# Low halves of every second granule of the up-projections' weights: an adding DMA in place of a subtraction on VectorE

## The chip, the cores and the metric

One core of a Trainium2 chip runs the whole program. The metric is the device time of one execution in microseconds (us), the median of several runs; smaller is better. Times of instructions, waits and transfers come from one profiled execution, whose own time is given beside its span.

## The reference

The program computes a small decoder trunk for 256 tokens of 2048 features in float32: an mLSTM layer, then a layer of differential attention, each followed by a gated feed-forward with a causal convolution over tokens, and a last RMS norm. The change touches the first product of the feed-forward, `xn @ w_up`:

```python
def conv_ffn(xn, w_up, conv_w, conv_b, w_down):
    S = xn.shape[1]
    u = xn @ w_up                       # (256, 2048) @ (2048, 11264)
    up = jnp.pad(u, ((0, 0), (CONV_W - 1, 0), (0, 0)))
    c = conv_b + up[:, 0:S] * conv_w[0]
    for j in range(1, CONV_W):
        c = c + up[:, j:j + S] * conv_w[j]
    gate, val = jnp.split(c, 2, axis=-1)
    return (jax.nn.silu(gate) * val) @ w_down

def reference(x, ...):
    h = x
    for layer in range(DEPTH):          # 2 layers
        ...
        h = h + conv_ffn(rms_norm(h, f_norm[layer]), w_up[layer], conv_w[layer], conv_b[layer], w_down[layer])
    return rms_norm(h, final_norm)
```

## The kernel before

**Products of halves.** A float32 number is split into a high half (rounded to the type `fp32r`, in which TensorE multiplies) and a low half (the number minus its high half). A product is then three: high by high, high by low and low by high. The activations `x` are split once for each layer's norm. The weights are read once and are split as they come.

**Tiles.** `gemm` (from L374) works on 256 columns of a weight matrix at a time, a *pair* of blocks of 128. For each pair it walks over the inner dimension in *granules* of 4 tiles of 128 rows (`HC` = 4). In the up-projection the inner dimension is 2048, so a pair has 4 granules, at `k0` = 0, 4, 8 and 12. A load brings two granules at once: `raw`, 128 partitions by 8 by 256 numbers, 1 MiB (L361). There are five `raw` buffers.

**Splitting a granule** (`granule`, L353 to L372). ScalarE copies the granule's part of `raw` into the high half of a buffer `w2` (L369), which rounds it. VectorE writes the low half as part minus high half (L371). There are five `w2` buffers (`HL` = 5), so the split runs up to four granules ahead of TensorE. In `w2` the high and low half of one tile of rows stand side by side: [128, 4 tiles, 2 halves, 256].

**The matmuls** (L411). For each tile of rows and each block of 128 columns there are two: the high half of the weights against high and low half of `x` side by side (512 wide), and the low half against the high half of `x` (256 wide). A granule of the up-projection has 16 matmuls, a pair 64. When a pair is done, ScalarE and VectorE add up the two halves of each accumulator (L417, L418), and the convolution follows on them (L656 to L673).

**The feed-forward** (`conv_ffn`, from L645). The 5632 hidden features are taken in two halves. For each half there are 22 pairs of the up-projection (11 of the gate, 11 of the value, alternating), then the down-projection. Two layers of two halves make four up-projection stages of 22 pairs: 88 pairs, 352 granules, 176 loads.

**Order and queues.** Every engine works through its own queue in order; the order is set when the program is built. Loads are all issued by SyncE, and wait until the last reader of a `raw` buffer is done. GpSimd issues no transfers. In the profile's names `w` is the tile `w2`, `x_f` the split activations of the feed-forward, `hid` the split hidden features.

Of the kernel before, what the change touches and what calls it, by code (L numbers as in the profile page):

```python
# [45 lines left out]
# 500000 ** (-i / 16) in float32, once for each half of a rotary pair  # L46
# [19 lines left out]
def trunk(  # L66
# [41 lines left out]
    # the tensor engine's clock rises with use: have it up when the first operands come  # L108
# [14 lines left out]
    # mask_a: row q, column k, NEG where k > q; mask_s: row s, column t, NEG where s > t; each twice  # L123
# [10 lines left out]
    def columns(sources, name):  # L134
        """rows of 128 parameters each, transposed: column j has parameters 128 j .. 128 j + 127"""
# [40 lines left out]
    def parameters():  # L176
# [3 lines left out]
        # w_hnorm / 2: the sigmoid of the output gate is (1 + tanh) / 2  # L180
# [7 lines left out]
    class Norm:  # L188
        """Sum of squares over the features, and the operands (h * gain) split in two exact halves."""
# [29 lines left out]
        def first(self, i, ps):  # L219
            """the same from the transposed input"""  # L220
# [11 lines left out]
        def rstd(self):  # L232
            """1 / sqrt(mean square + eps): rt per token on partitions, a column for each half of the tokens; r on every partition"""
# [16 lines left out]
    def sums(a):  # L250
        """the sums of a over the partitions: (P, 2), tokens on partitions, a column for each half of them"""
# [5 lines left out]
    def rsqrt(v, name, eng):  # L257
        """1 / sqrt(v) for (P, 2): a first guess from the exponent, then Newton's steps"""
# [17 lines left out]
    def spread(y):  # L276
        """(P, 2) with tokens on partitions to (P, T) with the same T tokens on every partition"""
# [25 lines left out]
    def split_weights(p, h_at, name):  # L303
        """(128, 384) of weights p[s, t] in two halves: columns 0-255 the first half of s against all t, columns 256-383 the second
        half of s against the second half of t. Three blocks of (h, l), in that order"""
# [11 lines left out]
    def weighted(v, p):  # L317
        """sum over s of p[s, t] v[s, :], a bank with t on partitions for each half of t"""
# [11 lines left out]
    def squares(banks):  # L330
        """the sum of squares of a head's 256 features, (P, 2)"""
# [12 lines left out]
    def turn(rows, name):  # L344
        """two (128 t, 256) to features on partitions, (2, T)"""
# [7 lines left out]
    def granule(w, c0, k0, kn, raws, j, hc=None, first=False, own=True):  # L353
        """the two halves of up to HC k-tiles of 256 columns; a load brings KC of them, at the very beginning HC"""
# [13 lines left out]
        w2 = wpool.tile([P, HC, 2, CW], F32R, tag="w2", name="w2", bufs=HL)  # L368
        splits.append(act.activation(w2[:, :hc, 0], part, AF.Copy))  # L369
        eng = pool if first and k0 // HC % 2 else dve  # L370
        eng.tensor_tensor(w2[:, :hc, 1], part, w2[:, :hc, 0].bitcast(F32), op=ALU.subtract)  # L371
        return [(w2[:, i, 0], w2[:, i, 1]) for i in range(hc)], w2  # L372

    def gemm(xs, w, col0, pairs, evac, tokens_out=False, lead=1, before=None, narrow=()):  # L374
        """256 columns of w at a time. Features out: ps[n] is (128 columns, T). tokens_out: ps[t] is (128 tokens, 256 columns).
        Every product is of two 12-bit halves: wh xh + wh xl + wl xh. wide: the first two are one matmul, of the two halves side by
        side, into the two halves of a bank, which are added up at the end.
        narrow: pairs without that.
        lead: the first so many pairs leave the last operands until all of them have used the others."""
# [7 lines left out]
        for j, k0 in order:  # L387
# [6 lines left out]
            halves, w2 = granule(w, c0, k0, kn, raws, j, ends[k0] - k0, before is not None)  # L394
            wide = j not in narrow
            for i, (wh, wl) in enumerate(halves):
                k = k0 + i
                xh, xl, xhl = xs[k]
                for n in range(2):
                    s = slice(n * P, (n + 1) * P)  # L400
                    one = ps[n][:, :T]
                    if wide and tokens_out:
                        ops = ((xh[:, s], w2[:, i].rearrange("p a n -> p (a n)"), ps[n]), (xl[:, s], wh, one))
# [18 lines left out]
    def gemm_by_tokens(xs, w, col0, evac):  # L422
        """256 columns of w, tokens out, the first half of the tokens ahead of the second"""
        kn, raws, halves = len(xs), {}, []
        ps = [acc_ps.tile([P, 2 * T], F32, tag="acc", name="acc")[:, :T] for _ in range(2)]
        for t in range(2):
            s = slice(t * P, (t + 1) * P)
            for k in range(kn):
                if t == 0 and k % HC == 0:
                    # the first HL granules in the weights' own buffers, the others in blocks that are free by now  # L430
# [36 lines left out]
    def x_squares():  # L467
        """the sum of squares per token"""
# [6 lines left out]
    def mlstm(norm):  # L475
# [5 lines left out]
        def gates():  # L481
            gw = wpool.tile([P, KC * CW], F32, tag="raw", name="gw", bufs=RAW)[:, :KD * 16].rearrange("p (k n) -> p k n", n=16)
            # the columns' first halves and, 64 columns on, their second halves
# [450 lines left out]
```

## Time and profile before

| | us |
|---|---|
| median of 3 runs | 2281.04 (2280.92 to 2281.47) |
| span of the profiled execution | 2280.0 |
| TensorE busy | 2267.8 |
| VectorE busy | 1588.7 |
| ScalarE busy | 1258.4 |
| GpSimd busy | 175.7 |
| DMA engines, mean rate | 183 GB/s |

The span is the time from the first to the last instruction of one profiled execution. PE is TensorE's matmuls, PEld its weight loads, DVE VectorE, ACT ScalarE, POOL GpSimd, SP SyncE; a "q" behind a name is the engine's sequencer. A row of the groups shows line, engine, operation, what is written from what, the shape and the count, then the busy time in all, the mean time of one in ns, and the engine's idle time just before with what ended it. A row of the busy times by stage shows the stretch, then the busy time and the count for each engine, then TensorE's granted clock, the busy share of the 16 DMA engines and their rate in GB/s. A row of the timeline shows start, duration and instruction, with the idle time before it in brackets.

### The profile page before, as it was taken

The page shows a single profiled execution, that of the slowest core. Times are in us where ns is not written, and L with a number is a line of the kernel's source. Part 1 is how long each engine was busy: PE and PEld are TensorE (multiplying, and loading weights), DVE is VectorE, ACT ScalarE, POOL GpSimd, SP SyncE. Part 2 cuts the span into 40 slices and gives each one's busy share as a digit, 9 for nine tenths or more (in the row PEclk, how much of TensorE's full clock was granted, in tenths as well). Part 3 has the DMA queues.
Part 4 walks back from the last instruction along what each step waited for, and adds up shares of the span by engine and source line. Part 5 has one row for each costly group of instructions (what it writes and reads, how often), then busy time and mean ns, then how long its engine had stood idle before and what let it go on. Part 6 is the DMA issues. An engine that isn't in the chain of part 4 may idle for free.

```text
span 2280.0 us, 34236 instructions
## 1 busy us (share of the span) xinstructions
PE 2267.8 (99%) x13318; PEld 1995.3 (88%) x13318; DVE 1588.7 (70%) x2667; ACT 1258.4 (55%) x2019; POOL 175.7 (8%) x379
## 2 busy tenths in 40 slices
PE   9999999999999999999999999999999999999998
PEld 8888888888888888888988888988888888888887
DVE  7756667777764677775588875677777556777755
ACT  6466555655554455655554556556555445555544
POOL 2023001000000000000122213210000000000000
PEclk9999999999999999999999999999999999999999
DMA  9654566555556655565656555555555565555552
GB/s 281 186 151 150 181 187 193 185 194 188 185 178 192 202 187 185 188 190 175 200 184 191 167 159 162 179 185 185 188 192 185 171 198 192 189 191 192 174 184 89
DMA packets 415783, 418.18 MB, mean 183 GB/s; under 512 B 9134, under 2 KB 415620, under 8 KB 415620
## 3 DMA queue, kind: packets, MB, share of 16 engines
q1 hardware_dynamic: 415620, 415.98, 57.6%
q8 instruction: 105, 1.72, 0.3%
q14 instruction: 58, 0.48, 0.1%
HBM read 413.86 MB, written 2.10 MB: 182 GB/s over the span
## 4 chain that ended last, share of the span: by engine, by line
PE 99%; DMA 1%; SPq 0%; DVE 0%; ACT 0%; issue 0%; DVEq 0%; ACTq 0%
PE acc L411 95%; PE val_ps L326 1%; PE acc L435 1%; DMA raw<-in_m_w_in_dram 0%; PE as_ps L759 0%; DMA x_raw<-in_x_dram 0%; PE w_ps L572 0%; PE gps L492 0%; PE as_ps L760 0%; PE hn_ps L350 0%; PE an_ps L350 0%; PE s_ps L579 0%; PE out_ps L863 0%; PE t_ps L781 0%; SPq L361 0%; SPq L460 0%
## 5 line engine op out<-in xcount | busy, mean ns | idle before, releaser
L371 DVE TENSOR_TENSOR w<-raw,w 128x1024 fp32r<-128x1024 f32 (+1 forms) x799 | 957.9, 1199 | 563.4 <-ACT w L369 560.5
L369 ACT ACTIVATE w<-raw 128x1024 fp32r<-128x1024 f32 (+1 forms) x803 | 833.1, 1038 | 759.8 <-PE acc L411 717.2
L411 PE MATMUL acc<-x_f,w 128*128 128x512 f32 (+1 forms) x5632 | 985.1, 337 | 0.0
L411 PEld LDWEIGHTS acc<-x_f,w 128*128 128x128 f32 x5632 | 861.0, 188 | 122.0
L411 PE MATMUL acc<-hid,w 128*128 128x512 f32 (+1 forms) x2772 | 481.5, 335 | 0.0
L411 PEld LDWEIGHTS acc<-hid,w 128*128 128x128 f32 x2772 | 420.4, 188 | 57.8
L417 ACT ACTIVATE low<-acc 128x256 f32<-128x256 f32 x354 | 129.6, 384 | 188.6 <-PE acc L411 188.3
L418 DVE TENSOR_TENSOR acc<-acc,low 128x256 f32<-128x256 f32 x354 | 138.4, 430 | 71.1 <-ACT low L417 71.1
L411 PE MATMUL acc<-x_a,w 128*128 128x256 f32 (+1 forms) x1056 | 186.0, 335 | 1.3 <-ACT w L369 0.7
L411 PE MATMUL acc<-x_at,w 128*128 128x512 f32 (+1 forms) x1024 | 181.5, 338 | 0.0
L411 PEld LDWEIGHTS acc<-x_a,w 128*128 128x128 f32 x1056 | 160.2, 190 | 22.9 <-DVE w L371 1.0
L411 PEld LDWEIGHTS acc<-x_at,w 128*128 128x128 f32 x1024 | 156.7, 188 | 21.9
L658 ACT ACTIVATE c<-u,conv 128x256 f32<-128x256 f32 x176 | 95.7, 592 | 0.0
L411 PE MATMUL acc<-w,x_a 128*128 128x512 f32 (+1 forms) x512 | 93.4, 340 | 0.0
L411 PE MATMUL acc<-w,x_at 128*128 128x256 f32 (+1 forms) x544 | 93.1, 329 | 0.0
L411 PE MATMUL acc<-ao,w 128*128 128x512 f32 (+1 forms) x576 | 91.0, 319 | 0.0
L411 PE MATMUL acc<-mo,w 128*128 128x256 f32 (+1 forms) x544 | 90.3, 327 | 0.0
L411 PEld LDWEIGHTS acc<-ao,w 128*128 128x128 f32 x576 | 81.7, 188 | 8.6
L411 PEld LDWEIGHTS acc<-mo,w 128*128 128x128 f32 x544 | 80.0, 188 | 9.8
L411 PEld LDWEIGHTS acc<-w,x_at 128*128 128x128 f32 x544 | 80.3, 188 | 9.2
L411 PEld LDWEIGHTS acc<-w,x_a 128*128 128x128 f32 x512 | 78.4, 188 | 10.7
L659 DVE SCALAR_TENSOR_TENSOR c<-u,conv,c 128x255 f32<-128x255 f32 x176 | 76.9, 478 | 0.0
(255 smaller groups left out, 1159.4 us busy)
## 6 DMA issues: line engine op xcount, KB each, us to landing
raw<-in_w_up_dram SPq DMA_DIRECT2D x176, 1024.0 KB
raw<-in_w_down_dram SPq DMA_DIRECT2D x64, 1024.0 KB
raw<-in_m_w_in_dram SPq DMA_DIRECT2D x46, 1024.0 KB
raw<-in_w_kv_dram SPq DMA_DIRECT2D x32, 1024.0 KB
raw<-in_w_down_dram SPq DMA_DIRECT2D x32, 768.0 KB
raw<-in_m_w_out_dram SPq DMA_DIRECT2D x16, 1024.0 KB
raw<-in_w_q_dram SPq DMA_DIRECT2D x16, 1024.0 KB
raw<-in_w_o_dram SPq DMA_DIRECT2D x16, 1024.0 KB
```

The source lines that it names most:

```text
L326: pe.matmul(ps[:, :vh.shape[1]], a, b, start=(s == 0 and o == 0), stop=(s == t and o == 2))
L369: splits.append(act.activation(w2[:, :hc, 0], part, AF.Copy))
L371: eng.tensor_tensor(w2[:, :hc, 1], part, w2[:, :hc, 0].bitcast(F32), op=ALU.subtract)
L411: pe.matmul(to, a, b, start=(k == 0 and o == 0), stop=(k == kn - 1 and o == len(ops) - 1))
L417: act.activation(low, p[:, T:], AF.Copy)
L418: dve.tensor_tensor(p[:, :T], p[:, :T], low, op=ALU.add)
L435: pe.matmul(ps[t], a[:, s], b, start=(k == 0 and o == 0), stop=(k == kn - 1 and o == 2))
L658: act.activation(c, u, AF.Identity, bias=cw[:, 3, f:f + 1], scale=cw[:, 2, f:f + 1])
L659: dve.scalar_tensor_tensor(c[:, 1:], u[:, :T - 1], cw[:, 1, f:f + 1], c[:, 1:], op0=ALU.mult, op1=ALU.add)
```

## The change

Three edits go together.

1. The buffer `w2` is laid out by half first: [128, 2 halves, 4 tiles, 256]. All stages use it. Where the tokens are the output's rows, the 512-wide operand is now two runs of 256 numbers that lie 4 KB apart.
2. In the four up-projection stages, every second granule (`k0` = 4 and 12, the second granule of each `raw`) gets its low half in another way: ScalarE writes the negated rounded part into the low half, and GpSimd issues a transfer that adds the part from `raw` to it.
3. The other granules of these stages, and all granules of the other stages, are split as before.

```diff
-        w2 = wpool.tile([P, HC, 2, CW], F32R, tag="w2", name="w2", bufs=HL)
-        splits.append(act.activation(w2[:, :hc, 0], part, AF.Copy))
-        eng = pool if first and k0 // HC % 2 else dve
-        eng.tensor_tensor(w2[:, :hc, 1], part, w2[:, :hc, 0].bitcast(F32), op=ALU.subtract)
-        return [(w2[:, i, 0], w2[:, i, 1]) for i in range(hc)], w2
+        w2 = wpool.tile([P, 2, HC, CW], F32R, tag="w2", name="w2", bufs=HL)
+        high, low = w2[:, 0, :hc], w2[:, 1, :hc]
+        splits.append(act.activation(high, part, AF.Copy))
+        if by_dma and k0 // HC % 2:
+
+            act.activation(low, part, AF.Copy, scale=-1.0)
+            pool.dma_start(low, part, accum_op=ALU.add)
+        else:
+            eng = pool if first and k0 // HC % 2 else dve
+            eng.tensor_tensor(low, part, high.bitcast(F32), op=ALU.subtract)
+        return [(w2[:, 0, i], w2[:, 1, i]) for i in range(hc)], w2
...
-                        ops = ((xh[:, s], w2[:, i].rearrange("p a n -> p (a n)"), ps[n]), (xl[:, s], wh, one))
+                        ops = ((xh[:, s], w2[:, :, i], ps[n]), (xl[:, s], wh, one))
...
-                gemm(norm.sets[0], w_up[layer], part * half * P, [j], evac_gate)
-                gemm(norm.sets[0], w_up[layer], D_FF + part * half * P, [j], evac_val)
+                gemm(norm.sets[0], w_up[layer], part * half * P, [j], evac_gate, by_dma=True)
+                gemm(norm.sets[0], w_up[layer], D_FF + part * half * P, [j], evac_val, by_dma=True)
```

ScalarE's queue in the first up-projection stage, one pair and the start of the next. L369 copies the high halves, L417 takes the upper half of an accumulator, L658 is the convolution, L291 splits the hidden features. Before:

```order
L417 ACTIVATE low<-acc 128x256 x2
L369 ACTIVATE w_4805<-raw 128x4x256
L658 ACTIVATE c<-u,conv_4043 128x256 x2
L369 ACTIVATE w_4824<-raw 128x4x256
L369 ACTIVATE w_4845<-raw 128x4x256
L291 ACTIVATE hid_4686<-c 128x256
L291 ACTIVATE hid_4696<-c 128x256
L369 ACTIVATE w_4864<-raw 128x4x256
L417 ACTIVATE low<-acc 128x256 x2
```

The same place with the change, where L370 is the high-half copy, L373 the negated one, L423 and L664 what L417 and L658 were:

```order
L423 ACTIVATE low<-acc 128x256 x2
L370 ACTIVATE w_4815<-raw 128x1024
L664 ACTIVATE c<-u,conv_4043 128x256 x2
L370 ACTIVATE w_4834<-raw 128x1024
L373 ACTIVATE w_4834<-raw 128x1024
L291 ACTIVATE hid_4694<-c 128x256
L291 ACTIVATE hid_4704<-c 128x256
L370 ACTIVATE w_4856<-raw 128x1024
L370 ACTIVATE w_4875<-raw 128x1024
L373 ACTIVATE w_4875<-raw 128x1024
L423 ACTIVATE low<-acc 128x256 x2
```

Each second granule's copy is followed at once by its negation; the evacuations and the split of the hidden features keep about their places around the copies.

SyncE's queue in the same stage, with what each load waits for. DVE and Activation stand for instructions of VectorE and ScalarE, DMAHW for an earlier transfer of SyncE's own, DMASW for one that GpSimd issued. Before:

```order
L361 DMA raw<-in_w_up_dram 128x8x256 [waits DMAHW5_49,DVE_49]
L361 DMA raw<-in_w_up_dram 128x8x256 [waits DMAHW6_49,DVE_49]
L361 DMA raw<-in_w_up_dram 128x8x256 [waits DMAHW7_49,DVE_49]
L361 DMA raw<-in_w_up_dram 128x8x256 [waits DMAHW0_49,DVE_49]
L361 DMA raw<-in_w_up_dram 128x8x256 [waits DMAHW1_49,DVE_49]
```

The same loads with the change:

```order
L361 DMA raw<-in_w_up_dram 128x8x256 [waits DMASW6_49,DMAHW5_49,DVE_49,Activation_49]
L361 DMA raw<-in_w_up_dram 128x8x256 [waits DMASW7_49,DMAHW6_49,DVE_49,Activation_49]
L361 DMA raw<-in_w_up_dram 128x8x256 [waits DMASW0_49,DMAHW7_49,DVE_49,Activation_49]
L361 DMA raw<-in_w_up_dram 128x8x256 [waits DMASW1_49,DMAHW0_49,DVE_49,Activation_49]
L361 DMA raw<-in_w_up_dram 128x8x256 [waits DMASW2_49,DMAHW1_49,DVE_49,Activation_49]
```

A load into a `raw` buffer now also waits for the adding transfer that reads this buffer. GpSimd's queue gets the 176 transfers themselves (L374), each behind the negated copy of its granule.

More of the change, by code (lines that the diff above doesn't have):

```diff
@@ L351, in turn, with granule @@
         return ps
-    def granule(w, c0, k0, kn, raws, j, hc=None, first=False, own=True):
+    def granule(w, c0, k0, kn, raws, j, hc=None, first=False, own=True, by_dma=False):
         at, hc = k0 % KC, hc or min(HC, kn - k0)
@@ L367, in granule, with gemm @@
             return pairs, None
-        w2 = wpool.tile([P, HC, 2, CW], F32R, tag="w2", name="w2", bufs=HL)
-        splits.append(act.activation(w2[:, :hc, 0], part, AF.Copy))
-        eng = pool if first and k0 // HC % 2 else dve
-        eng.tensor_tensor(w2[:, :hc, 1], part, w2[:, :hc, 0].bitcast(F32), op=ALU.subtract)
-        return [(w2[:, i, 0], w2[:, i, 1]) for i in range(hc)], w2
-    def gemm(xs, w, col0, pairs, evac, tokens_out=False, lead=1, before=None, narrow=()):
+        w2 = wpool.tile([P, 2, HC, CW], F32R, tag="w2", name="w2", bufs=HL)
[8 more added lines that the diff above has]
+        return [(w2[:, 0, i], w2[:, 1, i]) for i in range(hc)], w2
+    def gemm(xs, w, col0, pairs, evac, tokens_out=False, lead=1, before=None, narrow=(), by_dma=False):
         kn = len(xs)
@@ L393, in gemm @@
                 before(k0, ends[k0])
-            halves, w2 = granule(w, c0, k0, kn, raws, j, ends[k0] - k0, before is not None)
+            halves, w2 = granule(w, c0, k0, kn, raws, j, ends[k0] - k0, before is not None, by_dma=by_dma)
             wide = j not in narrow
```

## The prediction

> **What bounds the kernel now.** I read the page first, then the busy time by stage, then the timeline of one pair of column blocks, then SyncE's own waits.
>
> ```profile
> span 2280.0 us, 34236 instructions
> PE 2267.8 (99%) x13318; PEld 1995.3 (88%) x13318; DVE 1588.7 (70%) x2667; ACT 1258.4 (55%) x2019; POOL 175.7 (8%) x379
> ...
> PE 99%; DMA 1%; SPq 0%; DVE 0%; ACT 0%; issue 0%; DVEq 0%; ACTq 0%
> ```
>
> TensorE is busy for 2267.8 of 2280.0 us, and the chain that ended last is 99% matmuls. VectorE, whose work the change takes away, does not appear in that chain at all. The change acts in the four up-projection stages (two layers, two halves of the hidden features each); their busy times, one row for each stage and the sum:
>
> ```profile
> core 0: us, PE busy (x) PEld busy (x) DVE busy (x) ACT busy (x) POOL busy (x), PEclk, DMA share, GB/s
> 401.60:648.50 246.90, 246.90 (x1424) 216.59 (x1424) 187.36 (x327) 148.84 (x226) 1.80 (x2) 1.00 0.57 186
> 771.90:1017.20 245.30, 245.30 (x1411) 215.15 (x1410) 183.02 (x301) 143.13 (x217) 0.00 (x0) 1.00 0.57 187
> 1527.10:1774.30 247.20, 247.20 (x1419) 216.28 (x1418) 185.74 (x315) 145.25 (x220) 1.81 (x2) 1.00 0.57 185
> 1897.80:2144.10 246.30, 246.30 (x1411) 215.38 (x1410) 183.33 (x301) 143.45 (x217) 0.00 (x0) 1.00 0.58 186
> sum 985.70, PE 985.70 PEld 863.40 DVE 739.45 ACT 580.67 POOL 3.61; mean PE 246.43 PEld 215.85 DVE 184.86 ACT 145.17 POOL 0.90
> ```
>
> In these stages TensorE is never idle (985.70 of 985.70 us) and runs at the full granted clock (1.00). No faster other engine can shorten them. What can happen is that something else becomes slower than TensorE. Work is paced per load of 1 MiB (two granules); the page counts them:
>
> ```profile
> raw<-in_w_up_dram SPq DMA_DIRECT2D x176, 1024.0 KB
> ```
>
> 985.7 / 176 = **5.60 us of TensorE for each load**, 2.80 us for each granule. The DMA engines are at a share of 0.57: 0.57 x 5.60 = 3.19 us of each 5.60 are taken. The change adds to these engines and to ScalarE.
>
> **The change part by part.** Prices of the compute instructions:
>
> ```profile
> L371 DVE TENSOR_TENSOR w<-raw,w 128x1024 fp32r<-128x1024 f32 x764 | 933.3, 1222 | 559.3 <-ACT w L369 558.3
> L369 ACT ACTIVATE w<-raw 128x1024 fp32r<-128x1024 f32 x764 | 808.4, 1059 | 716.9 <-PE acc L411 678.4 <-issue 19.0 <-DMA raw<-in_m_w_in_dram 5.7
> ```
>
> *Removed:* 176 subtractions of 1.222 us, 215 us of VectorE. It was waiting for ScalarE between them (558.3 us in the row) and nobody on the path waited for it: gain 0.
>
> *Added on ScalarE:* 176 negated copies of the same shape, 176 x 1.06 = 187 us. In the stages ScalarE goes from 580.67 to 767 of 985.70 us, 78%. It keeps up; queued behind a negation are the next high-half copy and the evacuations of the accumulators, each up to 1.06 us later, and both have slack: the high-half copies start when TensorE frees a buffer, four granules before they are read. Cost 0 by itself; if that lead were gone it would be up to the whole 187 us.
>
> *Added on the DMA engines:* 176 accumulating transfers of 512 KiB (one granule, 4 KB in each partition), issued by GpSimd, which does next to nothing there (3.61 us), so nothing is queued behind it. The trace of before has neither an adding transfer nor one from GpSimd. That it uses the same engines is likely, since the page gives every queue as a share of the same 16:
>
> ```profile
> q1 hardware_dynamic: 415620, 415.98, 57.6%
> q8 instruction: 105, 1.72, 0.3%
> q14 instruction: 58, 0.48, 0.1%
> ```
>
> For the price of moving bytes I take the stretch in the middle of one load, where the engines are saturated:
>
> ```profile
> 901.60:904.20 2.60, 2.60 (x16) 2.27 (x16) 1.05 (x1) 1.06 (x1) 0.00 (x0) 1.00 1.03 357
> ```
>
> At 357 GB/s a load of 1.049 MB takes **2.94 us**. An adding transfer has three streams: the source is read, the old destination is read, the sum is written. For a load one read and one write run together as one pass, so bounds for the added transfer are: one pass of 512 KiB, 1.47 us, if the extra read costs nothing; two passes, 2.94 us, if the two reads follow one another; three passes, 4.41 us, if the write does not overlap either. I take **two passes, 2.94 us**: a load is read through one stream that is full at 357 GB/s, and there are twice as many bytes to read here. Then the engines need 2.94 + 2.94 = 5.88 us for each 5.60 us of TensorE. The excess is 0.28 us, 176 x 0.28 = **49 us**. The store of five raw and five split buffers covers only the first loads of a stage.
>
> *The wait that moves.* SyncE's loads are released by the last reader of a raw buffer:
>
> ```profile
> SPq L361 <- DVE w L371: 1372.6, 269, 10.8
> ```
>
> Now every second reader is the adding transfer, so in these stages a load leaves some microseconds later, once the transfer has landed. Behind it on SyncE's queue stand only the next loads. Five raw buffers hold 5 x 5.60 = 28 us of work, so this delay alone is hidden; when the engines are too slow it is the place where it shows.
>
> *The new latency.* One granule's split before:
>
> ```profile
> 903.13 1.06 ACT L369 ACTIVATE w<-raw 128x1024 fp32r<-128x1024 f32 x1 [1.73 <-PE acc L411]
> 904.22 1.23 DVE L371 TENSOR_TENSOR w<-raw,w 128x1024 fp32r<-128x1024 f32 x1 [1.56 <-ACT w L369]
> 905.47 6.18 SPq L361 DMA_DIRECT2D raw<-in_w_up_dram  x2
> ```
>
> ScalarE starts at 903.13, released by TensorE, the low half is there at 905.45, 2.3 us later, and SyncE's next load leaves at 905.47. TensorE reads it four granules, 11.2 us, after the release. Now two copies (2.12 us) and the transfer stand there. The nearest row for a transfer's whole latency is the last store, 256 KB, which follows this last row of the chain:
>
> ```profile
> 2275.07 0.39 DVE stream L893
> ```
>
> From its end, 2275.46, to the end of the span are 4.5 us, issue and landing included. The adding transfer has up to 1 MiB to read instead: 0.79 MB more at 357 GB/s, 2.2 us. In all 2.1 + 4.5 + 2.2 = 8.8 us, under 11.2: hidden on engines that are free, by 2.4 us; with a load in between (2.94 us) 11.8, which is not. That is the third rival below.
>
> *The buffers' layout* (all high halves, then all low halves) changes the addresses that every stage's matmuls read, not their number or shapes. Four stages of the same code take 245.3 to 247.2 us, 1.1 us or less from their mean; I take 0, with 4 x 1.1 = 4.5 us to either side.
>
> Sum: 2280.0 + 49 = 2329.0 us for a profiled execution; the median of the runs before is 1.0 us above its profile (2281.04), so **2330 us**.
>
> **The rivals.** *All hidden, not slower (2281 us).* It needs under 5.60 - 2.94 = 2.66 us of the engines for each adding transfer. For it: the one-pass bound gives 4.41 us a load, 79% of TensorE's time, and a packet here can be a partition's 4 KB, where the loads' are of 1 KB (415.98 MB in 415620 packets). Against it: the second read has to cost less than 81% of a pass.
>
> The Trainium skill, Collectives: The Full Stack, section The bandwidth ceiling: the fold count and why AG ≠ RS ≠ AR, states that the DMA engine's add itself is free and that a reduction runs at half a copy's rate because of its two source reads, about 31 GB/s for each engine and source. By that figure the 32 KiB of an engine would be an estimated 2.1 us, and 2.94 + 2.1 = 5.0 us would be hidden: 2281 us. No run here shows it yet.
>
> *The adding is slower than its reads (2589 us).* With three passes a load needs 7.35 us, 1.75 too many, 176 x 1.75 = 308 us. For it: a read-modify-write that cannot overlap. Against it: loads overlap read and write now.
>
> *Latency, not throughput (2323 us).* The engines have room, but the chain of 11.8 us is longer than the lead. A split buffer's cycle is then 2.8 us of reading plus 11.8, 14.6 instead of 5 x 2.8 = 14.0 us; 0.6 us for every five granules, 352 / 5 x 0.6 = 42 us. It decides only where the engines are not full; ScalarE's evacuations ahead of a copy make it worse.
>
> The Trainium skill, SBUF — State Buffer, section SBUF: two separate sides, adds that GpSimd cannot write a transfer's descriptors while VectorE runs in a mode that takes both ports. By it each transfer could start up to one VectorE instruction later, an estimated 1.2 us more of latency. VectorE's row above (1222 ns for 1024 elements, 1.2 ns each) does not suggest such a mode.
>
> *Faster (2271 us).* The layout suits TensorE's reads, and all its 2267.8 us shrink by what separates the fastest of the four stages from their mean (245.30 and 246.43, 0.46%): 10 us. Nothing in the rows speaks for it, and there is nothing else to win.
>
> **How the numbers follow.** Forecast (two passes) 0.40, all hidden 0.28, slow adding 0.17, latency 0.10, faster 0.05. Changes of 0.2% (4.6 us) count as a difference here. Slower by more: 0.40 + 0.17 + 0.10 = 0.67; within: 0.28; faster: 0.05. The forecast's own range is 2290 to 2418 us: its upper end prices both passes by the stage's mean share instead, 3.19 us a load, so 6.38 us, 0.78 too many, 137 us. The range of all cases, 2278 to 2540 us, holds the forecast, the hidden case and the latency; it leaves out most of the slow adding and the faster case, under 0.2.
>
> **What would show it.** If the forecast holds, the DMA share in the four windows rises from 0.57 to 0.95 or more, TensorE has idle time there that ends on the adding transfers, each stage takes 256 to 261 us instead of 246, and all other stages keep their times. A share of 0.85 with unbroken TensorE time means the second read was cheap. Idle TensorE with a share under 0.9 means latency. It is wrong if the transfers from GpSimd use something other than these 16 engines, or if one takes under 2.66 us of them.

## The result and the profile after

| | before | changed |
|---|---|---|
| median, us (five runs of each) | 2281.04 (2280.92 to 2281.47) | 2289.31 (2288.75 to 2292.71) |
| ratio, 95% interval | | 1.0038 [1.0025, 1.0052] |
| span of the profiled execution, us | 2280.0 | 2287.6 |

The change makes the kernel slower by 8.3 us, more than the 0.2% that can be told apart. The direction was forecast, the size was not: 8 us where 49 were worked out. (The table ahead of the prediction speaks of three runs of the kernel before; with the two taken beside the changed kernel there are five, with the same median.)

The page of the changed kernel, in the lines shown before:

```profile
span 2287.6 us, 35028 instructions
PE 2272.4 (99%) x13318; PEld 1996.0 (87%) x13318; DVE 1385.4 (61%) x2491; ACT 1419.7 (62%) x2195; POOL 330.1 (14%) x555
...
q1 hardware_dynamic: 415620, 415.98, 56.5%
q0 software_dynamic: 25344, 92.29, 21.6%
...
PE 95%; DMA 3%; issue 1%; SPq 0%; DVE 0%; ACT 0%; DVEq 0%; POOLq 0%; ACTq 0%
```

VectorE lost 203 us of work and ScalarE gained 161, and neither shows in the time. A new queue, `q0`, holds the adding transfers: 25344 packets, 144 for each of the 176 (128 of 4 KB and 16 of 4 bytes), and 21.6% of the engines' span. The chain of waits, 99% TensorE before, is now 95% TensorE and 3% DMA.

The busy times by stage, each from just before its first matmul to just behind its last:

```profile
400.20:649.20 249.00, 248.35 (x1424) 216.88 (x1423) 137.61 (x281) 186.20 (x268) 38.38 (x45) 1.00 1.04 276
772.40:1020.90 248.50, 247.27 (x1411) 215.56 (x1410) 133.26 (x258) 183.04 (x260) 37.02 (x43) 1.00 1.04 275
1530.70:1780.80 250.10, 248.30 (x1422) 216.64 (x1421) 137.65 (x273) 183.54 (x262) 38.65 (x45) 1.00 1.04 275
1903.80:2151.80 248.00, 247.09 (x1411) 215.61 (x1410) 133.57 (x258) 183.43 (x260) 37.00 (x43) 1.00 1.04 276
```

The engines' share went from 0.57 to 1.04, and the clock stayed at 1.00. That looks like full engines, and yet a stage takes some 2 us more, not 10 to 15. The groups of the up-projections' matmuls say how much of that is waiting. Before:

```profile
L411 PE MATMUL acc<-x_f,w 128*128 128x512 f32 (+1 forms) x5632 | 985.1, 337 | 0.0
```

and changed, with the adding transfers' own row:

```profile
L417 PE MATMUL acc<-x_f,w 128*128 128x256 f32 (+1 forms) x5632 | 989.5, 337 | 4.3 <-DMA w<-raw 4.1
L417 PEld LDWEIGHTS acc<-x_f,w 128*128 128x128 f32 x5632 | 861.6, 188 | 129.9 <-DMA w<-raw 6.9
...
L374 POOL DMA_DIRECT2D w<-raw x176 | 151.7, 862 | 1073.6 <-ACT w L373 592.2
```

The matmuls hold 4.4 us more busy time and 4.3 us of idle time, nearly all of the idle time ended by an adding transfer. The modelled end of a matmul hides part of a gap in "busy", so I count by the matmuls' starts, here and in the table of the experiments. A matmul of 512 columns is followed by the next start after some 232 ns, one of 256 after some 118 ns. What goes over that by more than 60 ns is called a gap; the rest I call the ordinary distances. The four stages have 7.0 us of gaps (0.3 before), and their ordinary distances are 2.3 us longer. Together the stages grow by 9.1 us. The first of them starts 1.25 us earlier (400.31, was 401.56), and the work between the third and the fourth is 0.3 us shorter. The difference is the span's 7.6 us. The early start is not the transfers' doing: with the layout alone (run 1 below) the first stage starts at 400.57.

Where two of the gaps come from, in the chain of waits of the changed kernel (start, duration, what):

```profile
789.78 2.46 PE acc L417 x14
792.24 0.03 POOLq L374
792.27 2.29 issue
794.55 0.01 POOLq L374
794.57 9.81 DMA w<-raw
804.37 0.04 issue
804.42 1.67 PE acc L417 x8
...
1668.13 9.22 DMA w<-raw
1677.35 0.04 issue
1677.39 2.73 PE acc L417 x15
```

The transfer that leaves at 794.57 lands 9.81 us later. TensorE freed its buffer at about 792.24, so the whole split took 12.1 us, against a lead of 11.2. All 176 together:

```profile
DMA to landing us min/median/max: 4.5/7.8/10.4
```

With the 2.4 us from the release to the issue (two copies and 0.3 us to GpSimd) the split takes 6.9, 10.2 and 12.8 us: most fit into the lead of 11.2, a few don't. SyncE's loads now wait for the adding transfers, as the prediction said, and no gap in these stages ends on a load of weights:

```profile
SPq L361 <- DMA w<-raw: 917.9, 175, 11.4
```

### The profile page after: what moved, and what is told of

The parts are those of the page before. It is cut to its first block, busy times and chain, and to the rows that moved or that the text cites. A ratio compares the mean times of both kernels' runs of the same rounds, so it can differ in the third digit from the quotient of the medians.

```text
span 2287.6 us, 35028 instructions
## 1 busy us (share of the span) xinstructions
PE 2272.4 (99%) x13318; PEld 1996.0 (87%) x13318; DVE 1385.4 (61%) x2491; ACT 1419.7 (62%) x2195; POOL 330.1 (14%) x555
## 3 DMA queue, kind: packets, MB, share of 16 engines
q0 software_dynamic: 25344, 92.29, 21.6%
## 4 chain that ended last, share of the span: by engine, by line
PE 95%; DMA 3%; issue 1%; SPq 0%; DVE 0%; ACT 0%; DVEq 0%; POOLq 0%; ACTq 0%
PE acc L417 92%; DMA w<-raw 2%; PE val_ps L326 1%; PE acc L441 1%; DMA raw<-in_m_w_in_dram 0%; PE as_ps L765 0%; DMA x_raw<-in_x_dram 0%; DMA rows<-in_conv_w_dram 0%; PE w_ps L578 0%; PE gps L498 0%; PE as_ps L766 0%; PE an_ps L350 0%; PE hn_ps L350 0%; PE s_ps L585 0%; PE out_ps L869 0%
## 5 line engine op out<-in xcount | busy, mean ns | idle before, releaser
L370 ACT ACTIVATE w<-raw 128x1024 fp32r<-128x1024 f32 (+1 forms) x803 | 832.9, 1038 | 666.4 <-PE acc L417 609.9
L377 DVE TENSOR_TENSOR w<-raw,w 128x1024 fp32r<-128x1024 f32 (+1 forms) x623 | 742.3, 1192 | 518.8 <-ACT w L370 516.2
L417 PE MATMUL acc<-x_f,w 128*128 128x256 f32 (+1 forms) x5632 | 989.5, 337 | 4.3 <-DMA w<-raw 4.1
L417 PEld LDWEIGHTS acc<-x_f,w 128*128 128x128 f32 x5632 | 861.6, 188 | 129.9 <-DMA w<-raw 6.9
L417 PE MATMUL acc<-hid,w 128*128 128x512 f32 (+1 forms) x2772 | 481.6, 335 | 0.0
L417 PEld LDWEIGHTS acc<-hid,w 128*128 128x128 f32 x2772 | 420.3, 188 | 57.9
L374 POOL DMA_DIRECT2D w<-raw x176 | 151.7, 862 | 1073.6 <-ACT w L373 592.2
L423 ACT ACTIVATE low<-acc 128x256 f32<-128x256 f32 x354 | 130.1, 385 | 130.7 <-PE acc L417 130.4
L417 PE MATMUL acc<-x_a,w 128*128 128x256 f32 (+1 forms) x1056 | 185.2, 335 | 0.2 <-DVE w L377 0.2
L373 ACT ACTIVATE w<-raw 128x1024 fp32r<-128x1024 f32 x176 | 183.5, 1042 | 0.0
L417 PE MATMUL acc<-x_at,w 128*128 128x512 f32 (+1 forms) x1024 | 181.5, 338 | 0.0
L417 PEld LDWEIGHTS acc<-x_a,w 128*128 128x128 f32 x1056 | 159.9, 190 | 21.4 <-DVE w L377 0.6
L417 PEld LDWEIGHTS acc<-x_at,w 128*128 128x128 f32 x1024 | 156.6, 188 | 21.9
L664 ACT ACTIVATE c<-u,conv 128x256 f32<-128x256 f32 x176 | 95.8, 592 | 0.2 <-DVE u L662 0.2
L417 PE MATMUL acc<-w,x_a 128*128 128x512 f32 (+1 forms) x512 | 93.4, 340 | 0.0
L417 PE MATMUL acc<-w,x_at 128*128 128x256 f32 (+1 forms) x544 | 93.1, 329 | 0.0
L417 PE MATMUL acc<-ao,w 128*128 128x512 f32 (+1 forms) x576 | 91.0, 319 | 0.0
L417 PE MATMUL acc<-mo,w 128*128 128x256 f32 (+1 forms) x544 | 90.5, 328 | 0.0
L417 PEld LDWEIGHTS acc<-ao,w 128*128 128x128 f32 x576 | 81.7, 188 | 8.6
L417 PEld LDWEIGHTS acc<-mo,w 128*128 128x128 f32 x544 | 80.1, 188 | 9.8
L417 PEld LDWEIGHTS acc<-w,x_at 128*128 128x128 f32 x544 | 80.3, 188 | 9.2
```

The source lines that it names most:

```text
L370: splits.append(act.activation(high, part, AF.Copy))
L373: act.activation(low, part, AF.Copy, scale=-1.0)
L374: pool.dma_start(low, part, accum_op=ALU.add)
L377: eng.tensor_tensor(low, part, high.bitcast(F32), op=ALU.subtract)
L417: pe.matmul(to, a, b, start=(k == 0 and o == 0), stop=(k == kn - 1 and o == len(ops) - 1))
L423: act.activation(low, p[:, T:], AF.Copy)
```

## The experiments

Eleven kernels, each compared with the kernel before on the same chip (2280.7 to 2281.0 us there). Lengths of the four stages in us, from the starts of their matmuls in the traces, against before:

| kernel | median | ratio | stages, us more than before | gaps over 60 ns |
|---|---|---|---|---|
| changed | 2289.31 | 1.0038 | +1.8 +3.1 +2.7 +1.5 | 7.0 |
| 1 layout alone | 2280.79 | 1.0001 | 0 0 0 0 | 0.3 |
| 2 plain copy | 2284.26 | 1.0015 | +0.4 +1.4 +0.4 +0.2 | 0.5 |
| 3 pieces of 1 KB | 2321.08 | 1.0175 | +10.8 +13.7 +13.1 +7.7 | 42.8 |
| 4 all granules | 2678.94 | 1.1754 | | 401 |
| 5 negations, no transfer | 2281.16 | 1.0001 | -0.3 0 0 0 | 0.3 |
| 6 every fourth granule | 2281.41 | 1.0003 | 0 0 0 0 | 0.4 |
| 7 six split, four raw buffers | 2287.53 | 1.0027 | +0.7 0 +3.8 0 | 4.9 |
| 8 five split, four raw buffers | 2300.05 | 1.0084 | +4.4 +7.0 +2.6 +2.9 | 14.8 |
| 9 late pairs alone | 2284.85 | 1.0019 | +1.6 +0.7 +1.7 +2.6 | 5.1 |
| 10 early pairs alone | 2285.61 | 1.0021 | +2.1 +1.1 +0.4 +1.1 | 4.6 |
| 11 order alone | 2285.79 | 1.0022 | +2.2 +2.5 +0.2 +0.2 | 0.3 |

The last two columns come from one profiled execution of each kernel. It need not be a typical one: run 9's is the slowest of its eleven (2287.49 us), and the executions of runs 7 and 8 spread over 7 and 12 us.

### 1. The layout alone

```diff
-                gemm(norm.sets[0], w_up[layer], part * half * P, [j], evac_gate, by_dma=True)
+                gemm(norm.sets[0], w_up[layer], part * half * P, [j], evac_gate, by_dma=False)
```

(and the same for the value pairs)

> The change without its transfers: new layout of the split buffers, all low halves subtracted by VectorE. Theory 'late transfers' (the changed kernel loses its 8 us where TensorE waits for adding transfers, 7.0 us in 21 gaps of the trace, and the layout costs nothing): 2279 to 2282 us. Rival 'layout' (the new addresses slow the matmuls; they pace 0.7 ns slower in the changed kernel, 983 to 985 us over the stages): 2283 to 2289 us.

2280.79 us, ratio 1.0001 [0.9992, 1.001]. All four stages have their old length to 0.01 us. The layout costs and brings nothing, so the loss belongs to the transfers and what comes with them.

### 2. A plain copy in place of the adding one

```diff
-            pool.dma_start(low, part, accum_op=ALU.add)
+            pool.dma_start(low.bitcast(F32), part)
```

> The 176 transfers copy the raw granule over the negated half instead of adding it, so the low halves are wrong (they hold the whole weight); instructions and their order are those of the changed kernel. Theory 'two reads' (an adding packet of 4 KB takes 328 ns of an engine because both operands are read): a packet takes 150 to 190 ns, the DMA share in the stages falls from 1.04 to about 0.8, the gaps go, 2279 to 2283 us. Rival 'one transfer from GpSimd costs the same whatever it does': packets of about 328 ns, 2289 us.

2284.26 us, ratio 1.0015 [1.0007, 1.0024], 1.3 us above the range of 'two reads'. The queue and one stretch in the first stage:

```profile
q0 software_dynamic: 25344, 92.29, 10.4%
```

```profile
460.00:640.00 180.00, 180.00 (x1031) 157.54 (x1030) 97.61 (x194) 133.85 (x194) 16.94 (x32) 1.00 0.85 281
```

Same packets, same bytes, same 281 GB/s, and half the time: 10.4% of 2281.6 us over 176 transfers is 1.35 us of every engine for each, where the adding one takes 21.6% of 2287.6 over 176, 2.81 us. A single 4 KB packet takes 159 ns plain and 328 ns adding (medians; eight of them on each engine). So adding costs a second pass. That it is the second read which takes it would fit the ratio; no run separates the read from the adding itself. With the short transfer the gaps are gone (0.5 us). About 2 us are left in the distances between matmuls; run 11 is about those. The profiled execution, the fastest of its eleven, has a span of 2281.6 us, 2.6 us more than run 1's on the same chip (2279.0), and 2.3 of them lie in the four stages. The 0.6 us from there to the median are not placed.

### 3. Pieces of 1 KB

```diff
-            pool.dma_start(low, part, accum_op=ALU.add)
+            pool.dma_start(low, part, accum_op=ALU.add, max_dma_last_dim=1024)
```

> The same adding transfers cut into packets of 1 KB instead of 4 KB, same order of instructions. Theory 'at the edge' (8 packets x 328 ns = 2.63 us of each engine for an add, and 2.94 us for a load, 5.57 us in all against 5.60 us of TensorE): any more engine time now shows in full. If an adding packet of 1 KB takes twice a load's 46 ns, 92 ns, an add takes 32 x 92 ns = 2.94 us, the sum is 5.88 us, and the kernel loses 176 x 0.28 = 49 us more or less: 2320 to 2340 us. Rival 'latency alone' (the engines have room, only the wait of single transfers hurts): under 2300 us.

2321.08 us, ratio 1.0175 [1.0159, 1.0191]. That is inside the range of 'at the edge', but by luck, as the page and the waits show:

```profile
span 2324.4 us, 35028 instructions
...
q0 software_dynamic: 92928, 92.29, 25.7%
```

```profile
PEld acc L417 <- DMA w<-raw: 44.0, 63, 2.5
PE acc L417 <- DMA w<-raw: 22.8, 33, 2.1
```

The same bytes in packets of 1 KB, 102 ns each, take 25.7% of 2324.4 us over 176, 3.39 us of an engine, 0.6 us more. The 0.6 us cost 0.23 us for each load (40.3 / 176): the rest still fitted. So the changed kernel has spare time on the engines, though little of it. By the expectation's own sum, with the 102 ns that were measured, an add would take 3.26 us and the kernel would lose 0.60 us for each load, 106 us; it lost 40.

### 4. Every granule by an adding transfer

```diff
-        if by_dma and k0 // HC % 2:
+        if by_dma:
```

> All 352 granules of the four stages get their low half by an adding transfer. Theory 'at the edge': a load and two adds need 2.94 + 2 x 2.63 = 8.20 us against 5.60, so 176 x 2.60 = 458 us more, about 2740 us. Rival 'latency alone': with twice the transfers, each issued earlier or later as before, not over 2350 us. ScalarE is at 93% then and stays below TensorE's time.

2678.94 us, ratio 1.1754 [1.1738, 1.177]. The queue, and the chain of waits by line (cut off by the view at its end):

```profile
q0 software_dynamic: 50688, 184.57, 34.6%
```

```profile
by line: PE acc L417 46.8%; DMA raw<-in_w_up_dram 42.1%; DMA raw<-in_w_down_dram 2.2%; DMA w<-raw 1.8%; issue 1.4%; PE val_ps L326 0.6%; ACT w L370 0.6%; PE acc L441 0.6%; DMA rows<-in_conv_w_dram 0.5%; PE as_ps L765 0.3%; DMA rows<-in_kv_n
```

Now the loads themselves are late: 42% of the chain. 398 us over 176 loads are 2.26 us, where 2.60 were expected. A load and two adding transfers need 5.60 + 2.26 = 7.86 us; an adding one here is 34.6% of 2685.7 us over 352, 2.64, and so 2.58 us are left for the load, or less if waits other than the engines have a part. (The granted clock fell to 0.943 in this run; the adding packets kept their 327 ns.) Run 3 gives 5.83 - 3.39 = 2.44 in the same way. Both are estimates, for packets of the two queues can run side by side on one engine, and the subtraction takes them one after the other. A load with the engines to itself is hardly faster than the prediction had it: in run 4 the loads move at most some 360 GB/s over 6 us, with next to nothing else on the engines, and that is 2.9 us for each.

### 5. The negation without the transfer

```diff
-            pool.dma_start(low, part, accum_op=ALU.add)
+            dve.tensor_tensor(low, part, high.bitcast(F32), op=ALU.subtract)
```

> ScalarE still writes the negated half in every second granule, but VectorE then makes the low half by subtraction and no transfer is issued. It asks what slows the matmuls by 2 us over the four stages (983.2 to 985.1 us by their pitch) in the changed kernel and in the one with plain transfers. Theory 'transfers' (the pitch falls when the DMA engines move more in SBUF): 983 us of pitch, 2280 to 2281.5 us. Rival 'ScalarE' (its extra writes do it): 985 us of pitch, 2282 to 2284 us.

2281.16 us, ratio 1.0001 [0.9992, 1.0009]. ScalarE's 176 negations cost nothing, in the matmuls' distances neither. That leaves the transfers, or what comes with them; runs 7 and 11 tell these apart.

### 6. Half as many adding transfers

```diff
-        if by_dma and k0 // HC % 2:
+        if by_dma and k0 // HC == 3:
```

> Only the last granule of each pair is made by an adding transfer: 88 instead of 176. Theory 'nearly full engines' (the gaps come because loads and adds together leave the engines a few per cent of room, so an add that is issued into a load queues for microseconds): the engines have 1.3 us more room for each load, the gaps nearly go, half of the pitch loss stays, 2281 to 2283 us. Rival 'every add is late when it meets a load' (the gaps scale with the number of transfers): half of the loss stays, 2284 to 2286 us.

2281.41 us, ratio 1.0003 [0.9995, 1.0012], and the transfers land sooner:

```profile
DMA to landing us min/median/max: 4.5/5.8/8.3
```

The longest split is then 2.4 + 8.3 = 10.7 us, inside the lead of 11.2, and TensorE waits nowhere. The ordinary distances, of whose growth half was expected to stay, are as before (984.7 us, 984.9 before). 88 adding transfers are free (ten of the eleven executions lie between 2280.8 and 2281.9 us, one at 2287.61); the loss isn't a price for each transfer.

### 7 and 8. One more split buffer

Run 7 has six split buffers and four raw ones (each of them holds 1 MiB). Run 8 is its control, with four raw buffers and the usual five.

```diff
-RAW = 5
+RAW = 4
-HL = 5
+HL = 6
```

> Six split buffers and four raw buffers instead of five and five: the split runs one granule further ahead, 2.8 us more time for each add. Theory 'latency at the start of the stages' (the longest adds land 10.4 us after their issue, the lead less the two copies is about 9 us): the gaps of 7 us go, 2281 to 2284 us. Rival 'throughput' (the engines are too slow on average): the gaps only come later, 2287 to 2292 us.

> Control for the run before: four raw buffers, the split buffers stay at five. Theory 'latency': as the changed kernel or a little worse, 2287 to 2294 us, since the lead of the split is the same. If this alone is at 2284 us or under, the raw buffers and not the lead made the difference: fewer loads are then in the queues ahead of an add.

Run 7: 2287.53 us, ratio 1.0027 [1.0018, 1.0036]. Run 8: 2300.05 us, 1.0084 [1.0072, 1.0097]. Run 7 missed the range of 'latency' (2281 to 2284 us) and lies in that of 'throughput'. Its trace speaks for latency all the same. Of its 4.9 us of gaps 1.0 lie at the very start of the first stage, where TensorE waits for the convolution's parameters and for no adding transfer, and 3.6 at one place in the third stage:

```profile
1666.00:1672.00 6.00, 4.17 (x15) 3.44 (x15) 5.62 (x11) 4.31 (x7) 1.72 (x2) 0.72 0.62 93
```

There TensorE waits 2.1 us for the 114th adding transfer, which leaves late for a reason of its own (see runs 9 and 10), and then the granted clock falls for 3.4 us, 0.72 in the mean of this stretch, which stretches the distances by another 1.5 us. The changed kernel pauses as long at its 114th transfer and keeps its clock at 1.00; what makes the difference is not shown. All other gaps of run 7 together are 0.3 us: with one granule more of lead no other adding transfer is late.

Against the control, with equal raw buffers, the sixth split buffer, 2.8 us of lead, takes back 12.5 us of the median. In the traces these are 9.9 us of gaps (14.8 to 4.9) and 2.5 us of ordinary distances, since the order on TensorE differs too (run 11). So the transfers' latency against the lead makes the gaps. The control was expected near the changed kernel's own time, at 2294 us at most, and missed that by 6 us, so the fifth raw buffer carries some of the load too. Six split and five raw buffers were not tried.

### 9 and 10. Only the late pairs, only the early pairs

In the changed kernel most gaps lie in the first 50 us behind a stage's first adding transfer. Is it the start of the stage, or the start of the transfers? So the adding transfers were kept out of the first six of a stage's 22 pairs (run 9), or allowed there alone (run 10):

```diff
-                gemm(norm.sets[0], w_up[layer], part * half * P, [j], evac_gate, by_dma=True)
+                gemm(norm.sets[0], w_up[layer], part * half * P, [j], evac_gate, by_dma=j >= 3)
```

(and the same for the value pairs; `j < 3` in run 10)

> The changed kernel with adding transfers only from the seventh of a stage's 22 pairs on (128 transfers instead of 176); the first 6 pairs, 34 us, are split by VectorE as before. Theory A (the gaps belong to the start of a stage, where the loads come in bursts and an adding transfer queues behind them): at most half of the changed kernel's 7.0 us of gaps is left, 3 us or less, and with the other order on TensorE (up to 2 us) the time is 2281 to 2285 us. Theory B (a start of its own: the adding transfers need some loads until they fall into step, wherever they begin): the gaps only move behind the first transfers, 5 to 8 us in all, and the time stays at 2286 to 2290 us.

> The other part alone: adding transfers only in the first 6 of a stage's 22 pairs (48 transfers). Theory A (start of a stage): the gaps of the first 60 us of the stages in the changed kernel, about 4 us of its 7.0, are all here, and the time is 2284 to 2287 us. If the gaps belong to long runs of adding transfers instead, they are under 1 us and the time is 2280 to 2282 us.

(The first six pairs take 67 us, 6 x 11.2; the 34 us in the expectation are a slip.) Run 10: 2285.61 us, ratio 1.0021 [1.0012, 1.0029], with 4.6 us of gaps. 3.1 us of them end on adding transfers, half of what the changed kernel has (6.2); 1.2 more end on the convolution's parameters at the start of the first stage. So the gaps do not belong to long runs of transfers.

Run 9: 2284.85 us, ratio 1.0019 [1.001, 1.0028], with 5.1 us of gaps. It does not decide between its theories. The time lies within A's range and under B's. The gaps are too many for A, but 2.4 us of them are one gap at the 114th transfer, with a cause of its own (below). The other 2.4 us follow the first adding transfers of the first and the third stage; the second and the fourth show none there. Two pieces of run 9's chain of waits:

```profile
480.26 9.59 DMA w<-raw
489.84 0.04 issue
489.89 2.13 PE acc L417 x11
...
1607.56 9.27 DMA w<-raw
1616.84 0.04 issue
1616.88 5.65 PE acc L417 x31
```

The first adding transfers of these two stages leave at 463.5 and 1590.7 us, and the first gaps end 26 us behind both. In the packets of the trace one can see how: the transfer of 480.26 gets its first packet only 5.0 us after its issue, and for most of that time the loads' packets keep the engines busy (a share of 0.96). In a stage's later part the transfers get theirs after some 1.7 us and run beside a load. In all four stages of run 9, and in all four of the changed kernel, some of the first ten transfers get their first packet more than 3 us after their issue. So wherever the adding transfers begin, they first run into the loads and then fall into step with them; that is theory B's picture. Whether TensorE then has to wait differs from stage to stage, and at the start of a stage it waits longer (4.3 us in the changed kernel, 2.4 in run 9), which is a part of A's.

The largest gap of run 9, 2.4 us at 2066, lies some 100 us behind the first transfer of its stage and has another cause, seen in the rows of ScalarE and GpSimd (start, duration, instruction, idle time before it):

```profile
2056.00 1.04 ACT L373 ACTIVATE w<-raw 128x1024 fp32r<-128x1024 f32 x1
...
2059.30 0.86 POOL L374 DMA_DIRECT2D w<-raw  x1 [6.70 <-DVE acc L424]
...
2061.63 1.04 ACT L373 ACTIVATE w<-raw 128x1024 fp32r<-128x1024 f32 x1
...
2062.99 0.86 POOL L374 DMA_DIRECT2D w<-raw  x1 [2.83 <-DVE c L679]
```

The negation at 2061.63 ends at 2062.67 and its transfer starts 0.3 us later, as nearly all do. The one before ended at 2057.04 and its transfer starts at 2059.30, 2.26 us later, though nothing that it waits for ended then; the releaser in brackets is the nearest event, not a cause. The changed kernel has the same behind its largest gap:

```profile
1659.24 1.04 ACT L373 ACTIVATE w<-raw 128x1024 fp32r<-128x1024 f32 x1
...
1660.58 0.86 POOL L374 DMA_DIRECT2D w<-raw  x1 [4.71 <-ACT c L672]
...
1664.83 1.04 ACT L373 ACTIVATE w<-raw 128x1024 fp32r<-128x1024 f32 x1
...
1668.13 0.86 POOL L374 DMA_DIRECT2D w<-raw  x1 [6.69 <-ACT w L370]
```

0.30 us, then 2.26 us. In both kernels it is the 114th adding transfer of the run, wherever it stands. The delay belongs to GpSimd's queue, by count, and not to the place (more on it at the end).

### 11. The order on TensorE, without transfers

In the trace of the changed kernel TensorE's matmuls come in another order at 74 of the 176 added granules. Before, a high-half matmul (512 columns wide) and a low-half one (256) alternate. Now, at 37 places, two high-half ones come before two low-half ones at the granule's start; at 37 others three high-half ones stand in a row, and the low-half ones that are left behind reach, as a rule, into the next pair. In runs 1, 5, 6 and 7 the two kinds alternate as before. Run 11 has the layout alone, with the first of these orders written out for all 176 granules (its expectation speaks of 111 places; 111 is how often a high-half matmul follows another at these 74):

```diff
+                if mixed and k0 // HC % 2 and i == 0:
+                    for n in range(2):
+                        pe.matmul(ps[n], wh[:, n * P:(n + 1) * P], xhl, start=False, stop=False)
+                    for n in range(2):
+                        pe.matmul(ps[n][:, :T], wl[:, n * P:(n + 1) * P], xh, start=False, stop=False)
+                    continue
```

(`mixed` is set in the up-projections)

> No adding transfer at all: the layout alone, with TensorE's first four matmuls of every second granule written in the order that the changed kernel shows at 111 places (both high-half ones, then both low-half ones) at 176 places. Theory (the order itself costs what the pitch shows, 1.9 us for 111 places): 3 us more than the layout alone, 2283 to 2285 us, at a pitch sum of 986 us. Rival (the longer pitch belongs to the transfers' traffic beside TensorE's reads): pitch sum 983 us and 2281 us, as the layout alone.

2285.79 us, ratio 1.0022 [1.0013, 1.0031]: 5.1 us with no transfer at all. One stretch of the first stage, before:

```profile
460.00:640.00 180.00, 180.00 (x1036) 157.89 (x1035) 136.06 (x228) 106.79 (x163) 0.00 (x0) 1.00 0.58 188
```

with this order:

```profile
460.00:640.00 180.00, 180.00 (x1025) 156.94 (x1024) 134.24 (x224) 105.13 (x161) 0.00 (x0) 1.00 0.58 186
```

and changed:

```profile
460.00:640.00 180.00, 180.00 (x1032) 157.48 (x1031) 97.61 (x195) 134.24 (x195) 27.52 (x32) 1.00 1.06 281
```

TensorE never pauses in any of the three, and gets through 1036, 1025 and 1032 matmuls. So the order costs time where no gap shows. It is dearer than expected (the ordinary distances grow by 5.0 us, not 3), and nearly all of it falls in the first layer (+2.2 and +2.5 us, against +0.2 twice). Nor does it stay at the granules whose order is new: in the first layer the four granules of a pair take 45, 20, 23 and 26 ns more, and only the second and the fourth were touched. In the second layer they take 0, 7, 0 and 0 ns more. What differs between the layers is open. In the changed kernel it is the same picture: of its 2.3 us, 1.9 lie in the pairs of the first layer that have a new order and 0.4 in those of the second; the other pairs take no longer than with the layout alone. By the count of places, 74 of 176, one would expect 2.1 us.

The rival, the transfers' traffic beside TensorE's reads, is settled by run 7: all 176 adding transfers, the old order, and ordinary distances of 984.7 us in the four stages (984.9 before, 987.2 in the changed kernel, 989.8 in run 11).

## Why the prediction was wrong in its size

**TensorE bounds, and VectorE's work is no gain:** right. 203 us less on VectorE bring nothing; the same subtraction in run 5 costs nothing.

**ScalarE's negations hidden, the layout 0, the later loads hidden:** right (runs 5, 1 and 6). The late release of raw buffers shows only where one of them is missing: run 8.

**Two passes for the adding transfer, excess 0.28 us for each load:** this is the step that failed, and by its size. That adding costs two passes holds: the adding packet takes 2.06 times a plain one (328 and 159 ns). The Trainium skill, Collectives: The Full Stack, section The bandwidth ceiling: the fold count and why AG ≠ RS ≠ AR, halves the rate of a reduction for its two source reads, and run 2's ratio agrees; by its rate of about 31 GB/s an adding transfer would be an estimated 2.1 us, and 2.64 to 2.81 us were measured. What was mis-sized is the sum 2.94 + 2.94. Both terms were read off one stretch at 357 GB/s, and they were put one behind the other. The adding transfer takes 2.64 to 2.81 us. Beside it a load takes an estimated 2.4 to 2.6 us of the engines (2.44 from run 3, 2.58 at most from run 4). Together that is 5.1 to 5.4 us for each 5.60 us of TensorE: over nine tenths full and not over the edge. Since a load alone was no faster than some 2.9 us, part of the room may come from packets of the two queues that run side by side, which the sum had at nothing; the runs don't separate this from a smaller price. The excess of 0.28 us was a small difference of nearly equal sums: a tenth off either term, or a twentieth off both, turns its sign. So there is no steady excess. That the kernel is slower all the same, as forecast, is luck: the loss has two other causes, one of them a rival's and one, the order on TensorE, that the sum had no term for. "All hidden" came nearest of the rivals: in the steady part of a stage it holds, and run 6 is that rival in full. It asked for under 2.66 us for the adding transfer; the 2.81 of the changed kernel are over that, and it is the load's smaller share that makes the room.

**What the share shows:** the prediction would have taken 0.95 or more for its proof. The share came out at 1.06 in a stretch without one pause of TensorE. It adds up the time of packets, and packets of two queues run side by side on one engine; above 1 it tells of sharing, not of a lack. Run 3, with 133 gaps, has 1.13 in the same stretch. The prediction's sign for latency, a share under 0.9, failed with it: the gaps are latency, and the share is 1.04.

**The latency rival** names the mechanism of the larger part of the loss, at the wrong price. It took 8.8 us for a split on free engines and 11.8 with a load in between. Measured are 6.9 at the least, 10.2 at the median, which is with a load running beside it, and 12.8 at the most. It charged 0.6 us for every five granules; in fact the median fits the lead, because in the steady part transfer and load run side by side (a transfer's first to last packet takes some 3 us where few packets of loads run beside it, and 5.8 beside a load), and only the ones that find a load's packets ahead of them wait up to 5.2 us for their first packet. These are mostly some of the first ten or so of a stage (runs 9 and 10); the others have fallen into step. That is a price for a few transfers, not for all. Runs 6 and 7 show it from both sides: less traffic, or more lead, and the gaps go or shrink.

**The account of the changed kernel,** from its trace: gaps 6.7 us more than before, of which 1.9 follow GpSimd's own delay at the 114th transfer, 4.3 are the other late ones and 0.5 end on the convolution's parameters at the start of the first stage; 2.3 us in the ordinary distances, for the order on TensorE; 1.25 us less by the earlier start of the first stage and 0.3 us less between the third and the fourth. Sum 7.5 us, where the span grew by 7.6 and the median by 8.3. That the 2.3 us are the order's is shown from both sides, by run 11 (one of the two orders, without transfers) and run 7 (the transfers without the order); the changed kernel with the strict order and five raw buffers was not run.

No kernel here beats the one before: with TensorE unbroken in these stages the best variants (runs 1, 5 and 6) equal it.

## What to carry to other kernels

Where two demands on a shared resource nearly equal the time that hides them, take each price from a run under that load, or say that the sign is open: here a tenth off either term turned it. Moving work from an engine off the critical path to the DMA engines gained nothing while TensorE bound, and it can lose through the latency of the first transfers and through another instruction order, long before the bandwidth is gone. After a change compare the order on the bounding engine as well: unbroken busy time can still hold fewer matmuls.

## What the runs showed of the hardware

- An adding transfer between SBUF tiles takes 328 ns of a DMA engine for a 4 KB packet, and 102 ns for 1 KB (3.26 us against 2.62 for 32 KB on each engine); a plain one of 4 KB takes 159 ns.
- GpSimd's transfers start 0.30 us after the negation ends, save at the 61st (0.97 us), the 114th (2.26 us) and the 167th (0.97 us), in every run with adding packets of 4 KB that gets that far: by count, every 53. With all granules added it goes on: 220th 2.26, 273rd 0.97, 326th 2.26 us. With packets of 1 KB it is 0.78 us every 24 transfers. The plain transfers of run 2 have it at the 114th alone (2.88 us). The cause is not shown.
- The Trainium skill, SBUF — State Buffer, section SBUF: two separate sides, lets VectorE hold up GpSimd's writing of descriptors while VectorE runs in a mode that takes both ports. No such delay shows here: 173 of 176 transfers start after the same 0.30 us, and the instruction that issues them takes 0.85 to 0.90 us in all but the first (1.07 us), though VectorE is at work for over 0.2 us of it in 89 cases. Whether VectorE's instructions here ever use such a mode, no run shows.
- Swapping the order of four matmuls in every 32 costs up to 2.5 us in a stage of 246 us, in one layer and not in the other, with no idle time anywhere in the records. More than half of it falls on granules whose own order is unchanged (run 11).
- After a pause of 2.1 us TensorE's granted clock fell for 3.4 us in run 7 (0.72 in the mean of 6 us); after pauses of 1.9 us in the changed kernel and 2.4 us in run 9 it did not.
